# MLP of a two-layer decoder trunk: Strassen product sums kept over the passes, a quarter of two more column blocks by Strassen, and PSUM banks named

## The chip, the core and the metric

The kernel runs on one core of a Trainium2 chip. The metric is device time in microseconds (us) of one execution, the median of several runs. The engines are PE (TensorE: matrix products), DVE (VectorE), ACT (ScalarE), POOL (GpSimd) and SP (SyncE, which here only issues transfers). PE writes its results to PSUM, eight banks of 128 partitions x 512 float32 numbers each; the other memory on the core is SBUF.

## The reference, cut to what matters

The model has two layers on one sequence of 256 positions with 2048 features. Layer 0 mixes by a gated short convolution, layer 1 by latent attention. Both have the same MLP behind the mixer, with its own weights, and a layer norm after every part:

```
def sq_relu_mlp(x, w1, w2):                    # w1: 2048 x 8192, w2: 8192 x 2048
    return jnp.square(jax.nn.relu(x @ w1)) @ w2

h = layer_norm(ALPHA * h + mix, ...)
h = layer_norm(ALPHA * h + sq_relu_mlp(h, mlp_w1[layer], mlp_w2[layer]), ...)
```

All data are float32.

## The kernel before, in words

**Numbers as pairs.** For a matrix product, each float32 operand is split in two parts, hi and lo, of the type fp32r. `split` (L114) does this: ACT writes hi by a cast (L116), DVE writes lo = x - hi (L117). A product a b is then taken as hi hi + hi lo + lo hi. With activations as the stationary operand and weights as the moving one, that is three matmuls of 512 columns, written by `dot` (L274 to L278). With weights as the stationary operand, one 512-column matmul takes hi of the weights against hi and lo of x side by side (`high`, L192), and one 256-column matmul takes lo against hi (`low`, L196).

**Weights.** All weights come through one list, `stream`, in tiles of 128 x 1024 (512 KB). `take` (L166) hands out the next ones and has `prepare` (L130) load and split tiles up to LOOK = 5 ahead. There are five buffers for raw tiles and eight each for hi and lo. The order of instructions on an engine follows the order of the program only roughly: the framework's scheduler places an instruction when its inputs and buffers are expected to be ready.

**The MLP** (`mlp`, L557) goes in 8 passes, q = 0 to 7. In a pass, `products` (L265) computes 8 chunks of 128 hidden features (16 K tiles each, ps_u), and `hidden` (L593) evicts each (`whole`, L329 to L333), applies the squared ReLU and splits the result. Then the down stage multiplies the pass's 8 chunks (K tiles, taken in 4 pairs) with the matching rows of w2 and adds the result to `acc`, which holds 2 row halves t x 4 column blocks n of 512. Pass 0 also finishes the norm before the MLP; in pass 7 the blocks go on to the next norm (`to_wide`) or to the output (`to_out`).

In passes 1 to 6 (FAST) the column blocks 0 and 1 are computed by Strassen's scheme in Winograd's form: per K pair, 7 factors in place of 8 block products (`down_fast`, ps_f). The weight side of the factors is made in `prepare` from two raw tiles (L130 to L160): three splits of 1024 columns, one of 512 (the tile t4), one subtraction of 1024 (L149) and two of 512 (L152, L155). The activation side is made in `hidden`: four sums of 128 columns (L605 to L608) and a split into `forms`. After four K pairs `combine` (L642) adds the seven products to `acc`, with 11 operations on DVE and one on ACT. Blocks 2 and 3 are computed plainly by `down` (L288): per K pair and block 2 x 2 x 3 = 12 matmuls (ps_d), and one addition to `acc` per row half (L581).

**Banks.** `psum` (L180) takes a PSUM tile from one of two pools of four buffers; a pool gives any free buffer. The second pool is closed in the attention part, where other tiles use its banks, and opened again after it (`banks = Banks.open("second")`), where `out_chunks` runs the rest of the attention's output projection (ps_l) behind its first three accumulators (ps_wo, `first_o`).

**Other lines that the text names.** `Norm.prepare` (L389) subtracts a mean taken from chunk 0, for which it needs one float32 matmul (mu0p, L396); `begin` calls it for all 16 chunks at the start of pass 7 of the first MLP. `residual` (L486, through L493) adds an accumulator to xres in two halves. `turn_residual` transposes the residual into `acc` in passes 1 to 4 of the second MLP. TURNED swaps `high` and `low` at the third K tile of a pass's first product. `to_out` loads the last gain and bias, gbt, by POOL's queue; the tables cos_t, sin_t and mask_t are loaded after the convolution.

Of the kernel before, what the change touches and what calls it, by code (L numbers as in the profile page):

```python
# [16 lines left out]
P = 128  # L17
# [5 lines left out]
NQ = 8  # L23
# [13 lines left out]
FAST = range(1, NQ - 1)  # L37
FIRST = (0, 1, 2, 4, 6, 8, 12, 16)
# [12 lines left out]
def trunk(ctx: ExitStack, tc: tile.TileContext, xT, vecs, w_first, w_in, w_out, w_kv, w_q, w_uk, w_uv,  # L51
          w_qn, w_qp, w_o, w1, w2, w2f, cosT, sinT, mask, ident, gb, out):
# [8 lines left out]
    pmm = ctx.enter_context(tc.tile_pool(name="pmm", bufs=4, space=PS))  # L61
# [12 lines left out]
    def mlp_stream(l):  # L74
        out = []
        for q in range(NQ):
            out += halves(w1[l, q * QC:(q + 1) * QC])
            lead = 0
            if q in FAST:
                out += [(w2f[l, q, j, 0], w2f[l, q, j, 1]) for j in range(QC // 2)]  # L80
                lead = 2
            out += halves(w2[l, q, lead:])
        return out
# [6 lines left out]
    class Banks:  # L90
# [4 lines left out]
        @classmethod  # L95
        def open(cls, name):
            st = ExitStack()
            cls.more, cls.count = st.enter_context(tc.tile_pool(name=name, bufs=4, space=PS)), 0
            return st
# [80 lines left out]
    def psum(name):  # L180
        return Banks.next().tile([P, 512], F32, tag="mm", name=name)
# [83 lines left out]
    def products(n, x, turned=None):  # L265

        for i in range(n):
            w = take()
            ps = psum("ps_u")
# [30 lines left out]
    def down_late(x, put, blocks):  # L300

        ws = {}
        for t in range(2):
            for n in blocks:
# [11 lines left out]
    def down_fast(x, forms):  # L316

        ps = {p: psum(f"ps_f{p}") for p, _, _ in FACTORS}
        n = len(x) // 2
        for j in range(n):  # L320
            b, = take(1)
            a = {"11": held(x[2 * j], 0), "12": held(x[2 * j + 1], 0), "22": held(x[2 * j + 1], 1)}
            for i in range(4):
                a[f"S{i + 1}"] = [forms[:, j, o, i * P:(i + 1) * P] for o in range(2)]
            for p, l, r in FACTORS:
                dot(ps[p], b[r], a[l], j == 0, j == n - 1)
        return ps
# [14 lines left out]
    cos_t = const.tile([P, T], F32, name="cos_t")  # L342
    sin_t = const.tile([P, T], F32, name="sin_t")
    mask_t = const.tile([P, 3 * P], F32, name="mask_t")
# [9 lines left out]

    def late_constants():
        nc.sync.dma_start(id_t, ident)
        nc.sync.dma_start(cos_t, cosT)
        nc.sync.dma_start(sin_t, sinT)
        nc.sync.dma_start(mask_t, mask)
# [193 lines left out]
    late_constants()  # L553
# [3 lines left out]
    def mlp(idx, ln, blocks, fast, begin=None, extra=None):  # L557
# [24 lines left out]

        for q in range(NQ):
# [5 lines left out]
            if q == NQ - 1 and begin:  # L589
                begin()  # L590
            pair = []

            def hidden(m, ps, evac, *func):  # L593
                f = tmp.tile([P, T], F32, tag="fh", name="fh", bufs=3)
# [4 lines left out]
                put_split(h[m], f)  # L599
                pair.append(f)  # L600
                if forms is not None and m % 2:
                    (a11, a21), (a12, a22) = ((v[:, :P], v[:, P:]) for v in pair[-2:])
# [8 lines left out]
            if q == 0:  # L611
                for m in range(QC):
# [12 lines left out]
                    if m > 0:  # L625
                        normal()
                acc = act.tile([P, 2, D], F32, tag="a1", name=f"acc{idx}")
            else:
                for m, ps in enumerate(products(QC, xhl, turned=None if q == NQ - 1 and begin else TURNED)):
                    hidden(m, ps, whole)  # L630

# [10 lines left out]
    def combine(put, p):  # L642

        put(0, 1, p["4"])
        put(0, 0, p["2"])
        put(1, 0, p["3"])
        v, u = (raws.tile([P, 2, BW], F32, tag="raw", name="vu")[:, i, :] for i in range(2))
        put(0, 0, p["1"])
        nc.scalar.copy(v, p["1"])
        nc.vector.tensor_tensor(v, v, p["6"], ALU.add)  # L650
        nc.vector.tensor_tensor(u, v, p["7"], ALU.add)
        put(1, 0, v)
        put(0, 1, u)
        put(1, 0, p["5"])
        put(1, 1, u)
        put(1, 1, p["5"])
# [23 lines left out]
    def prepare_all():  # L680
        for k in range(NC):
            ln.prepare(k)

    with tc.tile_pool(name="fast1", bufs=1) as fast:
        mlp(1, before, to_wide, fast, begin=prepare_all)


    with tc.tile_pool(name="att", bufs=1) as ap:
        lat = act.tile([P, 2 * NK, 2 * T], F32R, tag="c", name="lat")
        chl, qhl = ([lat[:, k, :] for k in range(o, o + NK)] for o in (0, NK))  # L690
        kpe = ap.tile([P, 2, T], F32, name="kpe")
# [6 lines left out]
        def rope(dst, src, rows):  # L698

            a = tmp.tile([P, T], F32, tag="sq", name="ropea")  # L700
            b = tmp.tile([P, T], F32, tag="nu", name="ropeb")
# [201 lines left out]
    def turn_residual(block, n):  # L903
        if 0 <= n < NB:
            for t in range(2):
                ps = psum("turned")
                for j in range(4):
# [155 lines left out]
```

## Time and profile before

| what | us |
|---|---|
| median of 3 runs (2032.22 to 2032.32) | 2032.28 |
| the profiled execution | 2031.86 |
| its span, first to last instruction | 2030.0 |
| PE busy, by the page | 2022.8 |
| DVE busy | 1637.1 |
| ACT busy | 1186.2 |
| bytes read from HBM | 381.25 MB |

The page's first part gives busy times. PE's is close to the span, but matmuls are pipelined and a busy PE need not be PE at its peak, so PE must also be read in order of time. In the same execution PE's work goes through these stages (start in us): first MLP, pass 1 products 454.47, Strassen part 498.86, plain part 518.45; pass 2 products 540.25; pass 7 products 969.4, down stage 1013.97; attention 1115.88 to 1249.77; second MLP, pass 1 products 1412.96; pass 7 products 1931.24, down stage 1975.63, last matmuls 2025. The granted clock of TensorE is 1.00 throughout. A row of the timeline shows start, length, engine, line, operation, what it writes and reads, and how many were merged into the row; in brackets, the idle time before it and what ended it.

### The profile page before, as it was taken

The numbers are of one execution on the slowest core, as the hardware profiler recorded it, in microseconds if no ns is written. First come the engines' busy times: TensorE is split into PE (matmuls) and PEld (weight loads), VectorE is DVE, ScalarE is ACT, GpSimd is POOL, SyncE is SP. The second block draws the span as 40 slices with busy tenths as digits, with TensorE's granted clock in tenths as the row PEclk, the third lists the DMA queues.
The fourth block names the chain that finished last, engine by engine and source line by source line (L and its number), as shares of the span: only waits on it lengthen the run. The fifth ranks groups of instructions, "written<-read, shape, count | busy, mean of one in ns | idle before, by whom it ended". The sixth has DMA issues, their size and how long they took to land.

```text
span 2030.0 us, 30192 instructions
## 1 busy us (share of the span) xinstructions
PE 2022.8 (100%) x11240; PEld 1763.4 (87%) x11240; DVE 1637.1 (81%) x2559; ACT 1186.2 (58%) x1849; POOL 4.5 (0%) x25
## 2 busy tenths in 40 slices
PE   9999999999999999999999999999999999999998
PEld 8888888988888888888889998898888888888886
DVE  7667677778898988989788978776889898898966
ACT  6444445676566565655656655566656656565661
POOL 0000000000000000000000000000000000000000
PEclk9999999999999999999999999999999999999999
DMA  8666666564746557465654544656474664746573
GB/s 307 209 191 187 188 190 193 162 210 138 251 148 216 193 170 256 145 229 174 232 176 153 177 129 137 195 168 205 136 240 155 213 204 164 250 143 221 190 228 121
DMA packets 106851, 385.32 MB, mean 190 GB/s; under 512 B 11856, under 2 KB 12752, under 8 KB 106448
## 3 DMA queue, kind: packets, MB, share of 16 engines
q1 hardware_dynamic: 105984, 381.17, 57.9%
q0 software_dynamic: 576, 2.10, 0.3%
q8 instruction: 88, 1.44, 0.3%
q14 instruction: 59, 0.48, 0.1%
q10 hardware_dynamic: 144, 0.13, 0.0%
HBM read 381.25 MB, written 2.10 MB: 189 GB/s over the span
## 4 chain that ended last, share of the span: by engine, by line
PE 99%; DMA 0%; DVE 0%; issue 0%; SPq 0%; ACT 0%; DVEq 0%
PE ps_u L192 20%; PE ps_l L192 13%; PE ps_u L196 11%; PE ps_d L276 7%; PE ps_d L277 7%; PE ps_d L278 7%; PE ps_l L196 7%; PE ps_f L278 4%; PE ps_f L276 4%; PE ps_f L277 4%; PE ps_w L226 1%; PE ps_w L224 1%; PE ps_w L225 1%; PE ps_g L226 1%; PE ps_g L224 1%; PE ps_g L225 1%
## 5 line engine op out<-in xcount | busy, mean ns | idle before, releaser
L117 DVE TENSOR_TENSOR lo<-raw,hi 128x1024 fp32r<-128x1024 f32 x710 | 858.7, 1222 | 271.5 <-ACT hi L116 199.9
L116 ACT CAST hi<-raw 128x1024 fp32r<-128x1024 f32 x710 | 740.9, 1050 | 428.4 <-DMA raw<-in_w_dram 134.6
L192 PE MATMUL ps_u<-xhl,hi 128*128 128x512 f32 x1792 | 621.3, 391 | 0.0
L196 PE MATMUL ps_u<-xhl,lo 128*128 128x256 f32 x1792 | 500.1, 280 | 0.0
L192 PEld LDWEIGHTS ps_u<-xhl,hi 128*128 128x128 f32 x1792 | 334.4, 187 | 71.9
L196 PEld LDWEIGHTS ps_u<-xhl,lo 128*128 128x128 f32 x1792 | 339.2, 189 | 1.7
L276 PE MATMUL ps_d<-hi,h 128*128 128x512 f32 x640 | 249.9, 390 | 0.0
L277 PE MATMUL ps_d<-lo,h 128*128 128x512 f32 x640 | 249.3, 390 | 0.0
L278 PE MATMUL ps_d<-hi,h 128*128 128x512 f32 x640 | 249.2, 389 | 0.0
L192 PE MATMUL ps_l<-xhl_a,hi 128*128 128x512 f32 x704 | 244.1, 393 | 0.0
L196 PE MATMUL ps_l<-xhl_a,lo 128*128 128x256 f32 x704 | 195.5, 280 | 0.0
L192 PEld LDWEIGHTS ps_l<-xhl_a,hi 128*128 128x128 f32 x704 | 132.2, 188 | 29.8
L278 PEld LDWEIGHTS ps_d<-hi,h 128*128 128x128 f32 x640 | 120.2, 188 | 25.2
L276 PEld LDWEIGHTS ps_d<-hi,h 128*128 128x128 f32 x640 | 120.2, 188 | 25.0
L277 PEld LDWEIGHTS ps_d<-lo,h 128*128 128x128 f32 x640 | 120.2, 188 | 24.6
L196 PEld LDWEIGHTS ps_l<-xhl_a,lo 128*128 128x128 f32 x704 | 131.9, 188 | 0.2
L597 ACT ACTIVATE fh<-fh 128x256 f32<-128x256 f32 x112 | 46.5, 415 | 89.2 <-DVE fh L333 89.1
L116 ACT CAST hi_t<-raw_t 128x1024 fp32r<-128x1024 f32 x48 | 50.6, 1054 | 55.5 <-DVE raw_t L149 30.5
L192 PE MATMUL ps_l<-z,hi 128*128 128x512 f32 x240 | 82.4, 391 | 0.0
L226 PE MATMUL ps_w<-xd,hi 128*128 128x258 f32 x256 | 72.7, 285 | 0.0
L224 PE MATMUL ps_w<-xd,hi 128*128 128x258 f32 x256 | 72.6, 284 | 0.0
L225 PE MATMUL ps_w<-xd,lo 128*128 128x258 f32 x256 | 72.4, 283 | 0.0
(253 smaller groups left out, 3185.1 us busy)
## 6 DMA issues: line engine op xcount, KB each, us to landing
raw<-in_w_dram SPq DMA_DIRECT2D x416, 512.0 KB, 4.3
raw<-in_w2f_dram SPq DMA_DIRECT2D x96, 512.0 KB, 3.5
raw<-in_w_in_dram SPq DMA_DIRECT2D x88, 512.0 KB, 3.8
raw<-in_w_out_dram SPq DMA_DIRECT2D x32, 512.0 KB, 3.6
raw<-in_w_o_dram SPq DMA_DIRECT2D x32, 512.0 KB, 4.0
raw<-in_w_kv_dram SPq DMA_DIRECT2D x10, 512.0 KB, 3.6
raw<-in_w_q_dram SPq DMA_DIRECT2D x8, 512.0 KB, 4.4
raw<-in_w_uk_dram SPq DMA_DIRECT2D x8, 512.0 KB, 4.6
```

The lines of the kernel that those rows point to most:

```text
L116: nc.scalar.copy(hi, src)
L117: nc.vector.tensor_tensor(lo, src, hi.bitcast(F32), ALU.subtract)
L192: nc.tensor.matmul(ps, w[blk // 8][0][:, blk % 8, :], x, start=first, stop=False)
L196: nc.tensor.matmul(ps[:, :T], w[blk // 8][1][:, blk % 8, :], x[:, :T], start=False, stop=last)
L224: nc.tensor.matmul(ps[:, :W], hi, x[k][:, :W], start=k == 0, stop=False)
L225: nc.tensor.matmul(ps[:, :W], lo, x[k][:, :W], start=False, stop=False)
L226: nc.tensor.matmul(ps[:, :W], hi, x[k][:, W:], start=False, stop=k == NC - 1)
L276: nc.tensor.matmul(ps, x[0], w[0], start=first, stop=False)
L277: nc.tensor.matmul(ps, x[0], w[1], start=False, stop=False)
L278: nc.tensor.matmul(ps, x[1], w[0], start=False, stop=last)
L597: nc.scalar.activation(f, f, AF.Relu)
```

## The change

1. In passes 1 to 6, one of the four K pairs of blocks 2 and 3 (the third: MIXED = "ppsp") is computed by the seven factors; the other three stay plain. Weights for it come in a new array w2g, in the same bytes.
2. The products are no longer combined in every pass. Each product has a place where it is summed over the passes: 1, 5, 7 and 6 in a new tile `sums`, 2, 3, 4 and the plain sum 22 in `acc` (`keep`). `fold` adds them up once per MLP, in 8 operations of 1024 columns during the products of pass 7.
3. Every PSUM tile has a bank by number. Tiles without a named bank take the next number of a count, modulo 8, or 4 while the second pool is closed. The products of passes 1 to 7 alternate between banks 0 and 1; the factors take 2 to 7 and 0, in the order 3, 1, 5, 7, 2, 6, 4.
4. Two chunks of hidden features are split together (512 columns) in passes 1 to 6.
5. The mean's matmul and chunk 0 of `begin` go to the end of pass 0's products; the other chunks go one or two at a time behind the products of pass 7. `turn_residual` runs after the first K pair of the plain part. Only pass 1 keeps the turned order.
6. For room in SBUF, the three tables are loaded when attention starts, gbt is loaded by SP's queue, and the scratch for POOL's transfers is made smaller.

```
+MIXED = "ppsp"
...
-    pmm = ctx.enter_context(tc.tile_pool(name="pmm", bufs=4, space=PS))
+    pmm = ctx.enter_context(tc.tile_pool(name="pmm", bufs=1, space=PS))
...
         def next(cls):
             cls.count += 1
-            return cls.more if cls.more is not None and cls.count % 8 >= 4 else pmm
+            return (cls.count - 1) % (4 if cls.more is None else 8)
...
-    def psum(name):
-        return Banks.next().tile([P, 512], F32, tag="mm", name=name)
+    def psum(name, bank=None):
+        bank = Banks.next() if bank is None else bank
+        return (pmm if bank < 4 else Banks.more).tile([P, 512], F32, tag=f"mm{bank}", name=name)
...
-    FACTORS = (("4", "22", "T4"), ("2", "12", "21"), ("3", "S4", "22"), ("1", "11", "11"),
-               ("6", "S2", "T2"), ("7", "S3", "T3"), ("5", "S1", "T1"))
+    OWN, KEPT = ("1", "5", "7", "6"), (2, 3, 4, 5, 6, 7, 0)
+    FACTORS = (("3", "S4", "22"), ("1", "11", "11"), ("5", "S1", "T1"), ("7", "S3", "T3"),
+               ("2", "12", "21"), ("6", "S2", "T2"), ("4", "22", "T4"))
...
+        def keep(p, g, ps):
+            at = sums[:, OWN.index(p), g, :] if p in OWN else \
+                block(*{"2": (2 * g, 0), "3": (2 * g + 1, 0), "4": (2 * g, 1), "22": (2 * g + 1, 1)}[p])
+            if q == 1 and p in OWN:
+                nc.scalar.copy(at, ps)
+            else:
+                nc.vector.tensor_tensor(at, at, ps, ALU.add)
+
+        def down_pairs(h, forms):
+            n = QC // 2
+            ps = {p: psum(f"ps_f{p}", bank) for (p, _, _), bank in zip(FACTORS, KEPT)}
+            for j in range(n):
+                fast_products(ps, h, forms, j, ps if j == 0 else (), ps if j == n - 1 else ())
+            for p in ps:
+                keep(p, 0, ps[p])
+            ps = {p: psum("ps_d", bank) for p, bank in zip(("22", "3", "2", "4"), (1, *KEPT))}
+            for j, kind in enumerate(MIXED):
+                if kind == "s":
+                    first, last = j == MIXED.index("s"), j == MIXED.rindex("s")
+                    if first:
+                        ps.update({p: psum(f"ps_f{p}", bank) for p, bank in zip(OWN, KEPT[3:])})
+                    fast_products(ps, h, forms, j, OWN if first else (), OWN if last else ())
+                    if last:
+                        for p in OWN:
+                            keep(p, 1, ps[p])
+                    continue
+                for nb, two in ((3, ((1, "22"), (0, "3"))), (2, ((0, "2"), (1, "4")))):
+                    w, = take(1)
+                    for t, p in two:
+                        for kk in range(2):
+                            k = 2 * j + kk
+                            dot(ps[p], wide_rows(w, kk), held(h[k], t), k == 0, k == QC - 1)
+                if extra and q <= NB and j == 0:
+                    for t in range(2):
+                        extra(block, q - 1, t, KEPT[4 + t])
+            for p in ("3", "2", "4", "22"):
+                keep(p, 1, ps[p])
+
+        def fold():
+            s1, s5, s7, s6 = (sums[:, i] for i in range(4))
+            c = acc.rearrange("p t (g b c) -> p t b g c", g=2, b=2)
+            for d, a, b in ((c[:, 0, 0], c[:, 0, 0], s1), (s6, s6, s1), (c[:, 0, 1], c[:, 0, 1], s6), (s7, s7, s6),
+                            (c[:, 1, 0], c[:, 1, 0], s7), (c[:, 1, 1], c[:, 1, 1], s7),
+                            (c[:, 0, 1], c[:, 0, 1], s5), (c[:, 1, 1], c[:, 1, 1], s5)):
+                nc.vector.tensor_tensor(d, a, b, ALU.add)
+                yield
...
-                for m, ps in enumerate(products(QC, xhl, turned=None if q == NQ - 1 and begin else TURNED)):
+                folds = fold()
+                for m, ps in enumerate(products(QC, xhl, TURNED if q == 1 else None, (0, 1))):
                     hidden(m, ps, whole)
+                    if q == NQ - 1:
+                        next(folds)
+                        if begin:
+                            begin(range(max(2 * m, 1), 2 * m + 2))
...
             if q in FAST:
-                combine(put, down_fast(h, forms))
-            for n in range(2 if q in FAST else 0, NB):
-                if n == NB - 1 and extra:
-                    extra(block, q - 1)
-                down(h, put, n)
+                down_pairs(h, forms)
+            else:
+                for n in range(NB):
+                    down(h, put, n)
...
-            nc.gpsimd.dma_start(gbt[:, n, :], gb[n].partition_broadcast(P))
+            nc.sync.dma_start(gbt[:, n, :], gb[n].partition_broadcast(P))
```

More of the change, by code (lines that the diff above doesn't have):

```diff
@@ L263, in opening, with products @@
         yield from [ps for _, ps in ws]
[L265 removed]
+    def products(n, x, turned=None, banks=(None,)):
         for i in range(n):
             w = take()
[L269 removed]
+            ps = psum("ps_u", banks[i % len(banks)])
             mm_run([(w, ps)], x, 0, NC, NC, turned=None if i else turned)
```

113 lines of the change are left out of this document (53 added, 60 removed).

## The prediction, made before the changed kernel ran

> **What bounds the kernel now.** I read the page's busy times first, then the chain that ended last, the waits of PE, and then PE's instructions in order of time.
>
> ```profile
> span 2030.0 us, 30192 instructions
> ...
> PE 2022.8 (100%) x11240; PEld 1763.4 (87%) x11240; DVE 1637.1 (81%) x2559; ACT 1186.2 (58%) x1849; POOL 4.5 (0%) x25
> ...
> PE 99%; DMA 0%; DVE 0%; issue 0%; SPq 0%; ACT 0%; DVEq 0%
> ```
>
> PE is busy for the whole span and is 99% of the chain. The four waits of PE that the profile names come to 3.2 us, and none lies in an MLP pass. So only fewer or faster matmuls can help, and any new wait of PE costs its full length. But the 390 ns of a matmul in the groups is latency, not price: the next one starts long before it ends. The price is the distance from start to start.
>
> ```profile
> 498.86 0.39 PE L276 MATMUL ps_f<-t,h 128*128 128x512 f32 x1
> ...
> 518.45 0.40 PE L276 MATMUL ps_d<-hi,h 128*128 128x512 f32 x1
> ...
> 540.25 0.39 PE L192 MATMUL ps_u<-xhl,hi 128*128 128x512 f32 x1
> ```
>
> These are the first Strassen matmul of pass 1 of the first MLP, its first plain one (ps_d) and the first product of pass 2. Between them lie 84 Strassen matmuls, 19.59/84 = **0.2332 us** each, and 96 plain ones, 21.80/96 = **0.2271 us** each. (At 390 ns each removed matmul would count 1.7 times.) A pass is 44.39 + 19.59 + 21.80 = 85.78 us, and the passes between repeat this to 0.02 us (the second MLP has 0.9 us more in four of them, for transposes). There are 12 such passes (q 1 to 6, twice). The next question is what DVE has left in each stage of a pass:
>
> ```profile
> 626.03:670.42 44.39, 44.39 (x257) 39.17 (x256) 36.79 (x57) 29.07 (x49) 0.00 (x0) 1.00 0.51 166
> 670.42:690.01 19.59, 19.59 (x86) 15.78 (x85) 18.38 (x26) 12.47 (x18) 0.00 (x0) 1.00 0.60 193
> 690.01:711.81 21.80, 21.80 (x98) 18.02 (x96) 19.32 (x23) 10.87 (x11) 0.00 (x0) 1.00 0.76 252
> ```
>
> The rows are products, Strassen part and plain part of pass 3; after the length come the busy times of PE, PEld, DVE, ACT and POOL. DVE is idle for 7.6, 1.2 and 2.5 us. The cover is there, but in the Strassen part it is thin.
>
> **Step 1, the removed matmuls.** One of four K pairs of blocks 2 and 3 goes from 2 x 2 x 2 x 3 = 24 plain matmuls to 7 x 3 = 21. At the rows' prices this is 24 x 0.2271 - 21 x 0.2332 = 5.450 - 4.897 = 0.553 us a pass, 12 x 0.553 = **-6.6 us**. The changed order (six plain matmuls to a bank, the factor T4 last) has no row. If the new Strassen matmuls ran at the plain price, 3 x 0.2271 x 12 = -8.2 us. If all 72 plain ones of a pass rose to the Strassen price, 12 x 72 x 0.0061 = 5.3 us would be lost again and -1.3 us left. I take -6.6, each kind at its own row. The Trainium skill, "TensorE: Matmul & The Clock Gate", section "Wait — 56ns, not 53.3ns?", gives one spacing of 215.7 ns for all warm 512-column matmuls; by it step 1 would be an estimated 36 x 0.2157 = 7.8 us. The trace has two spacings, both longer.
>
> **Step 2, DVE in a pass.** Back to back, an operation of 1024 columns takes 1.14 us (four in a row 4.63 us, one 1.22), of 512 columns 0.60 (two 1.28, one 0.68), of 256 columns 0.34 (four 1.43, one 0.42). Removed: two plain splits (2.27), 11 operations of combine and 4 puts. Added: a Strassen pair, 4 x 1.14 + 3 x 0.60 = 6.35, and 15 keeps in place of those 15 operations. The split by pairs gives 4 x 0.60 for 8 x 0.34, -0.3. Net +3.8 us: from 74.5 to 78.3 us in a pass of 85.2. It fits on the whole, so I cost it at nothing; the work that hides it is PE's. In the part after the first four pairs DVE needs 19.3 + 4.1 = 23.4 us against 21.2 of PE. The 2.2 us over spill into the next products, which have 7.6 to spare, and eight hi/lo buffers carry them. The mixed pair sits third, so PE wants its first factor 2 x 5.45 = 10.9 us after the first four pairs and its last, T4, 4.2 us later, at 15.1. From that start DVE owes 7 keeps (4.2), one plain split (three already ran in the last 5 us of the Strassen part: 684.47, 3.69 us for three) and for the first factor one split of the pair: 4.2 + 1.1 + 1.1 = 6.4 of 10.9 us; for all of the pair 4.2 + 1.1 + 6.35 = 11.7 of 15.1. ACT gains about 1 us on 52.4 and stays clear. If the cover is gone, each us late costs 12.
>
> **Step 3, the banks.** Products now have two banks, so the eviction of product m must end within one product, 5.55 us. In the passes shown here the eviction (L333) ends 2.1 to 4.0 us after its product. Of the first keeps, the banks of 3, 1 and 5 are wanted again 1.4, 2.7 and 4.1 us after the Strassen part ends; today the first three evictions end 1.3 us before, 1.6 and 3.3 us after it. The slack is 1.5, 1.1 and 0.8 us. In four passes of the second MLP the transposes want the fifth and sixth at 5.45 and 5.85 us; at 0.6 us a keep they end near 4.5 and 5.1. So nothing, but barely.
>
> One bank does collide. Before, a slot is taken from a pool of four; afterwards the number is a count modulo 4 or 8, set to 0 when the second set of banks opens. Counted through the code, 49 tiles in the convolution, 16 in its output, 19 in q 0 of the first MLP (the mean's included), 19 in q 7, 10 in the latent stage, 49 in attention: 162. The three w_o accumulators are 163 to 165, banks 2, 3 and 0; the next product is tile 1 of the new count, bank 0. It has to wait for the third accumulator's eviction.
>
> ```profile
> 1249.64 0.28 PE L196 MATMUL ps_wo<-oT,lo 128*128 128x256 f32 x1
> 1249.77 1.99 PE L192 MATMUL ps_l<-oT,hi 128*128 128x512 f32 x8
> ```
>
> ```profile
> 1249.26 1.43 DVE L493 TENSOR_TENSOR xres<-xres,ps_wo 128x256 f32<-128x256 f32 x4 [1.56 <-PE ps_wo L196]
> ...
> 1250.81 0.41 DVE L493 TENSOR_TENSOR xres<-xres,ps_wo 128x256 f32<-128x256 f32 x1
> ...
> 1251.47 0.42 DVE L493 TENSOR_TENSOR xres<-xres,ps_wo 128x256 f32<-128x256 f32 x1
> ```
>
> PE goes on at 1249.77 today; the last read of the third accumulator ends at 1251.89. The wait is 2.1 us, once: **+2.1**. Bounds: 0 if PE has the bank already, 2.5 with the signal's way. Behind it PE has only matmuls of that stage.
>
> **Step 4, what moves.** The mean's matmul (mu0p) goes from the start of q 7 to the end of q 0. Today a product's first pair after it takes 0.42 us instead of 0.23 (969.40 to 969.82); a plain matmul after transposes takes 0.32 (1036.56 to 1036.88). So -0.1. Unit 0 of q 2 to 7 loses its turned order; no row shows the unturned one after ps_d. From 0 (no gap there to win) to 0.19 x 11 = +2.1, the gap after mu0p as upper end; I take 0, since the gap stands only behind 32-bit matmuls. The fold is 8 x 1.14 = 9.1 us of DVE in each q 7, one step to a product: splits 2.3 + evictions 0.7 + step 1.1 + two prepares 0.7 = 4.8 of 5.55 us. The four loads of gbt go to SP's queue, where they wait for the last product (1975.6) with weight loads behind them. At that moment SP issues the 11th of q 7's 16 plain tiles, 30 us ahead of PE at 2.73 us a tile; gbt lands in 7.4 to 12.4 us. Nothing; if SP reached them six tiles earlier, about 1 us. The tables cos, sin and mask load (4.9 us) into memory that is free before q 7's down stage and are used 50 us later.
>
> **Sum.** -6.6 + 2.1 - 0.1 = -4.6 us. The profiled execution took 2031.86 (span 2030.0 and 1.8 around it) and gives 2027.3; the median of the runs is 0.4 higher, so 2032.3 - 4.6 = **2027.7**. About 0.2% (4.1 us, the line is 2028.2) is what a measurement of this kernel can tell from no change, and the forecast lies just past it.
>
> **Rivals.**
> - **A, the forecast**: 2027.7, own range 2026 to 2029.8. 0.55, of which 0.42 below 2028.2.
> - **B, no wait at w_o**, or Strassen at the plain price: 2032.3 - 6.7 = 2025.6, down to 2024. For: DVE may do the third accumulator's adds first. Against: the row above. 0.13.
> - **C, a wait in every fast pass**: the mixed pair's weights, or a bank, come late. For: DVE has 1.2 us idle in the Strassen part, and the tightest slack above is 0.8 us, at a bank. Against: the pair has 3.4 us to spare, and today's passes run at this density without a wait. 1.0 us late in each gives 12 more: 2039.7. It decides from 4.6/12 = 0.38 us a pass on; from 0.72 the kernel is slower by over 0.2%. 0.15. By the section "A second HAM failure mode: psum-queue depth-cycling" of the same page of the Trainium skill, short idle times between groups that cycle through banks also let the clock drop; here the clock is 1.00 in all three rows, and that time would come on top.
> - **D, unturned starts**: +2.1, 2029.8. 0.05.
> - **E, the removal does not pay**: the plain matmuls take the Strassen price, -1.3 + 2.0 = 2033. For: the reason of the 6 ns is not in the trace. Against: plain matmuls keep 0.2271 in all passes. 0.12, of which 0.09 within 0.2%.
>
> Faster 0.42 + 0.13 = 0.55; within 0.13 + 0.05 + 0.09 = 0.27; slower 0.15 + 0.03 = 0.18. The range goes from 2023.5 (all of B) to 2034.5 (past E); C is left out.
>
> **What would show it.** A pass should be 85.2 us, 44.4 + 19.6 + 21.2, without a gap in PE (A, B) or with one at the mixed pair, at a bank's first matmul or at the third product (C). Between ps_wo and ps_l PE should stand 2.1 us. The start distances decide E, unit 0 of a pass decides D. I would be wrong above all if PE waits in every pass.

## The result, and the profile after

The changed kernel takes 2036.57 us (median of 15 runs, 2034.0 to 2040.39), the kernel before 2031.88 us beside it (15 runs, 2031.42 to 2033.58). The ratio is 1.0024, with a 95% interval of 1.0016 to 1.0032: slower by about 0.2%, and outside the range of the prediction. The profiled execution took 2035.76 us.

The page of the changed kernel, its first part and its chain:

```profile
span 2034.0 us, 30032 instructions
...
PE 2025.4 (100%) x11204; PEld 1756.3 (86%) x11204; DVE 1686.9 (83%) x2571; ACT 1198.7 (59%) x1829; POOL 2.3 (0%) x21
...
PE 93%; DVE 4%; DMA 1%; issue 1%; ACT 1%; DVEq 0%; ACTq 0%
```

There are 36 matmuls fewer (11204 for 11240), and PE is busy for 2.6 us longer. So the rest must have become dearer. DVE and the transfers now have 5% of the chain, so PE waits for them here and there. The waits of PE, as engine, line and releaser, then us in total, times, longest:

```profile
PE ps_u L199 <- DVE sums L588: 1.9, 3, 1.0
PE offset L1011 <- DVE udiag L1009: 1.4, 1, 1.4
PE warm L353 <- DVE col L355: 1.1, 1, 1.1
PE ps_d L283 <- DVE sums L588: 0.2, 1, 0.2
```

The first and the last row are new. There PE wants a bank whose keep (L588) DVE has not finished. With PE's rows in order of time these are five gaps in the second MLP, 2.9 us in all. That is less than the span grew, so the next view is the length of each stage. Stretches of the changed kernel (products, Strassen part and the rest of pass 2, then the attention's projection behind ps_wo); after the length come the busy times of PE, PEld, DVE, ACT and POOL, the clock, DMA share and GB/s:

```profile
539.94:585.15 45.21, 45.21 (x257) 39.23 (x256) 38.70 (x58) 27.69 (x45) 0.00 (x0) 1.00 0.54 171
585.15:604.64 19.49, 19.49 (x87) 15.81 (x86) 17.74 (x24) 12.85 (x17) 0.00 (x0) 1.00 0.62 193
604.64:625.90 21.26, 21.26 (x94) 17.47 (x93) 20.30 (x24) 11.08 (x12) 0.00 (x0) 1.00 0.69 238
1250.38:1323.77 73.39, 73.39 (x419) 63.72 (x418) 59.99 (x100) 40.95 (x59) 0.00 (x0) 1.00 0.61 190
```

and two of the same stages before:

```profile
540.25:584.64 44.39, 44.39 (x257) 39.17 (x256) 37.35 (x59) 28.88 (x49) 0.00 (x0) 1.00 0.52 166
1249.77:1321.89 72.12, 72.12 (x419) 63.59 (x418) 59.29 (x100) 40.89 (x59) 0.00 (x0) 1.00 0.61 194
```

The down stage got shorter as meant, 19.49 + 21.26 = 40.75 for 41.39 us. But the products, 256 matmuls of which the change touches only the banks and the order of two at the start, take 45.21 for 44.39, with PE busy throughout, no wait and a clock of 1.00. The attention's projection, where only the banks changed, takes 73.39 for 72.12. The sum over the profiled execution:

| what | us |
|---|---|
| 12 down stages, 0.64 shorter each | -7.7 |
| 9 product stages of 14 at 45.2 to 45.3, some 0.82 longer each | +7.4 |
| projection behind ps_wo | +1.3 |
| five waits for keeps in the second MLP | +2.9 |
| sum (the span grew by 4.0) | +3.9 |

**Two rhythms.** Most of the gain was eaten by a rhythm of PE. These are the distances from start to start that the trace holds for the beginning of pass 2, in ns; the bar is the first product, L marks a 256-column matmul (`low`), the others have 512 columns:

```
before ... 226 227 227 | 226 114L 232 118L 121L 237 235 117L 235 116L 230 117L 230 117L ...
after  ... 227 226 227 | 227 113L 233 117L 241 120L 236 113L 233 117L 241 120L 236 113L ...
```

Both start alike. Before, the third K tile is turned (low ahead of high), and after two more pairs all pairs are 230 + 117 = 347 ns, or 1 ns less; their mean is 346.7 ns. Unturned, three pairs of 349, 350 and 361 ns repeat to the end of the stage; the mean is 353.3 ns. 128 pairs x 6.6 ns = 0.85 us, close to the row's 0.82. I call them the short and the long rhythm.

### The profile page after: what moved, and what is told of

Same layout as the page of the kernel before. It is cut to its first block, busy times and chain, and to the rows that moved or that the text cites. A ratio compares the mean times of both kernels' runs of the same rounds, so it can differ in the third digit from the quotient of the medians.

```text
span 2034.0 us, 30032 instructions
## 1 busy us (share of the span) xinstructions
PE 2025.4 (100%) x11204; PEld 1756.3 (86%) x11204; DVE 1686.9 (83%) x2571; ACT 1198.7 (59%) x1829; POOL 2.3 (0%) x21
## 4 chain that ended last, share of the span: by engine, by line
PE 93%; DVE 4%; DMA 1%; issue 1%; ACT 1%; DVEq 0%; ACTq 0%
PE ps_u L199 20%; PE ps_l L199 13%; PE ps_u L203 10%; PE ps_l L203 7%; PE ps_d L283 6%; PE ps_d L285 6%; PE ps_d L284 6%; PE ps_f L283 3%; PE ps_f L285 3%; PE ps_f L284 3%; PE ps_w L233 2%; PE ps_w L231 2%; PE ps_w L232 2%; DMA raw<-in_w_dram 1%; DVE lo L122 1%; PE ps_g L233 1%
## 5 line engine op out<-in xcount | busy, mean ns | idle before, releaser
L199 PE MATMUL ps_u<-xhl,hi 128*128 128x512 f32 x1792 | 629.6, 396 | 1.9 <-DVE sums L588 1.9
L283 PE MATMUL ps_d<-hi,h 128*128 128x512 f32 x556 | 217.5, 391 | 0.2 <-DVE sums L588 0.2
L285 PE MATMUL ps_d<-hi,h 128*128 128x512 f32 x556 | 216.6, 390 | 0.0
L284 PE MATMUL ps_d<-lo,h 128*128 128x512 f32 x556 | 216.6, 390 | 0.0
L121 ACT CAST hi_t<-raw_t 128x1024 fp32r<-128x1024 f32 x60 | 63.0, 1050 | 108.8 <-DVE raw_t L154 93.3
L283 PEld LDWEIGHTS ps_d<-hi,h 128*128 128x128 f32 x556 | 104.4, 188 | 22.6 <-DVE sums L588 0.7
L285 PEld LDWEIGHTS ps_d<-hi,h 128*128 128x128 f32 x556 | 104.4, 188 | 22.1
L284 PEld LDWEIGHTS ps_d<-lo,h 128*128 128x128 f32 x556 | 104.4, 188 | 21.7
L652 ACT ACTIVATE fp<-fp 128x256 f32<-128x256 f32 x96 | 40.0, 417 | 81.5 <-DVE fp L338 80.7
L154 DVE TENSOR_TENSOR raw_t<-raw,raw 128x1024 f32<-128x1024 f32 x60 | 73.1, 1219 | 7.4 <-DMA raw<-in_w2f_dram 7.3
L122 DVE TENSOR_TENSOR lo_t<-raw_t,hi_t 128x1024 fp32r<-128x1024 f32 x60 | 73.2, 1220 | 1.3
L233 PE MATMUL ps_w<-xd,hi 128*128 128x258 f32 x256 | 72.9, 285 | 0.0
```

Source lines behind the costliest of these rows:

```text
L121: nc.scalar.copy(hi, src)
L122: nc.vector.tensor_tensor(lo, src, hi.bitcast(F32), ALU.subtract)
L154: nc.vector.tensor_tensor(t.rearrange(two, a=2), b12.unsqueeze(1).to_broadcast([P, 2, BW]), r1.rearrange(two, a=2), ALU.subtract)
L199: nc.tensor.matmul(ps, w[blk // 8][0][:, blk % 8, :], x, start=first, stop=False)
L233: nc.tensor.matmul(ps[:, :W], hi, x[k][:, W:], start=False, stop=k == NC - 1)
L283: nc.tensor.matmul(ps, x[0], w[0], start=first, stop=False)
```

## The experiments

Theory S: the long rhythm, which an unturned start out of the even stream of plain matmuls (227 ns each) falls into, eats the gain. Theory W: the waits for late keeps do. Times are medians, with the range and the number of runs; ratios are to the kernel before, on the same chip, with a 95% interval. Of a changed line, only the part that differs is shown; `...` stands for lines left out.

**1. All passes turned again.**

```
-products(QC, xhl, TURNED if q == 1 else None, (0, 1))
+products(QC, xhl, TURNED, (0, 1))
```

> The changed kernel with the turned order kept for the first product of every pass from 1 to 7, not of pass 1 alone. Theory S (spacing): products that start unturned straight after 512-column matmuls run a whole stage at 45.21 us, turned ones at 44.39; all 14 product stages then read 44.4. In the profile of the changed kernel 9 stages were slow, so -9 x 0.82 = -7.4 us: 2036.6 becomes about 2029. Theory W (waits): the loss is PE waiting for late keeps at the end of passes of the second MLP, 2.8 us in the profile and more in other runs; turning changes nothing there, 2036.6 +- 1, and the scatter over the runs (2034 to 2040) stays.

2034.22 us (2031.27 to 2037.41, 11 runs), ratio 1.0009 (1.0 to 1.0018). This lies between the two. Eleven of the 14 stages are at 44.4 to 44.5 us, so turning does what S says; but gaps of 3.7 us stay, and three stages of the first MLP (passes 5 to 7) are still long. Passes 4 and 5, as stretches:

```profile
711.15:755.54 44.39, 44.39 (x257) 39.11 (x256) 39.50 (x58) 29.42 (x47) 0.00 (x0) 1.00 0.54 187
796.30:841.52 45.22, 45.22 (x257) 39.21 (x257) 40.49 (x59) 30.01 (x47) 0.00 (x0) 1.00 0.57 189
```

Both are turned. In the second one, two distances at the start are 3 to 4 ns longer. Its first two pairs are already those of the short rhythm, and the same turn leads out of it into the long one:

```
pass 5 ... 227 227 230 | 231 117L 230 117L 118L 232 231 114L 232 118L 240 120L 236 114L ...
```

So the rhythm hangs on the phase at which the turn meets it, and S and W are not independent: pass 7 is long behind a wait of 0.1 us.

**2. Another order of banks for the mixed pair's products**, so that bank 0, which the next products want first, holds the product whose keep comes first.

```
-zip(OWN, KEPT[3:])
+zip(("6", "5", "7", "1"), KEPT[3:])
```

> The changed kernel with one pair of banks exchanged: of the mixed pair's own products, the one that is kept first (1) takes bank 0, which the next pass's first product needs, and the one kept last (6) takes bank 5. Theory W: the waits of PE for keeps at the start of passes go, 2.8 us or more, and the runs scatter less: about 2033. Theory S: without a gap ahead of them, passes 3, 4 and 6 of the second MLP fall into the slow spacing too, 3 x 0.76 = 2.3 us, so the gain is eaten: 2036 +- 1, with 12 of 14 product stages at 45.2 us.

2036.58 us (2034.89 to 2037.41, 11), 1.0021 (1.0012 to 1.003). No gain, as S said. The waits ahead of the products are gone; but 12 stages are now long where there were nine, since a wait ahead of an unturned start had put it into the short rhythm three times. What the removed waits had cost, the longer stages took. Of the waits that stay, the two longer ones (0.6 and 1.2 us) lie in the plain part, for bank 3, the first keep of product 1; one of 0.16 us lies at the second product of a pass.

**3. The change without its mixed pair.** All four pairs plain; the second half of `sums` is zeroed.

```
-MIXED = "ppsp"
+MIXED = "pppp"
+        nc.gpsimd.memset(sums[:, :, 1, :], 0.0)
```

> The changed kernel with all four K pairs of blocks 2 and 3 plain (sums of the mixed pair set to zero once and folded like the others). It isolates the mixed pair. If its three matmuls fewer are worth what the plain part showed (21.26 us in place of 21.80, 0.54 a pass), passes lose 12 x 0.54 = 6.5 us. DVE has 4 us less a pass, so by W the waits of 2.8 us go: 2036.6 + 6.5 - 2.8 = 2040. By S the second MLP's stages behind those waits turn slow as well, +2.3: 2042.5. If mixing itself were the loss, the time would fall below 2036.

2042.13 us (2041.42 to 2045.0, 5), 1.0053 (1.0039 to 1.0067). As S says, 12 of 14 stages are at 45.21, and the gaps come to 0.24 us in all. The long rhythm does not need the mixed pair. And the mixed pair is worth its saving where nothing waits: a pass of the first MLP with the long rhythm takes 86.48 us here and 85.96 us in the changed kernel.

**4. The kernel before, unturned.**

```
-turned=None if q == NQ - 1 and begin else TURNED
+turned=TURNED if q == 1 else None
```

> The kernel before with one edit: only pass 1 keeps the turned order. Theory S: 11 more stages start unturned (pass 7 of the first MLP already did, behind the 32-bit matmul of the mean) and each goes from 44.39 to 45.21 us: 2031.9 + 11 x 0.82 = 2040.9. The prediction's upper end for this edit was 0.19 x 11 = 2.1, 2034. Theory W: no late keeps in this kernel, no change, 2031.9.

2040.34 us (2040.12 to 2042.87, 5), 1.0043 (1.0031 to 1.0056), where S expected 2040.9. The products of pass 2:

```profile
540.25:585.46 45.21, 45.21 (x257) 39.16 (x256) 38.26 (x60) 29.62 (x50) 0.00 (x0) 1.00 0.52 170
```

One edit, which adds no instruction, costs 8.3 us: eleven stages are at 45.21. In the traces the order of instructions on DVE and ACT is that of the kernel before, and on PE only the swaps differ. So S is shown in a kernel that has nothing else of the change.

**5. The change mended:** turned everywhere, the banks of 2, and fixed banks for ps_wo, so that the first ps_l is not blocked.

```
-first_o.append((take(), psum("ps_wo")))
+first_o.append((take(), psum("ps_wo", (2, 3, 1)[i])))
+                Banks.count += 2
```

> The changed kernel with three edits: turned order in every pass, the exchange of banks 0 and 5 among the mixed pair's products, and banks 2, 3 and 1 for the three w_o accumulators so that the next product finds bank 0 free. If slow spacing and late keeps together are the whole loss: 9 stages back to 44.4 (-7.4), w_o stage back from 73.4 to 72.1 (-1.3), part of the 2.8 us of waits: 2036.6 - 8.7 - 1 = 2027. What the earlier run with the turned order alone leaves open is whether a wait of a few ns ahead of a turned start also leads to the slow spacing; if so, up to four stages stay at 45.2: 2030. If the loss lies elsewhere, it stays above 2034.

2032.55 us (2028.18 to 2033.6, 11), 0.9997 (0.9988 to 1.0006). All 14 stages are at 44.39 and the projection is at 72.12 again, yet the time is that of before. In the profiled execution, the shortest of the eleven, the new row among PE's waits is:

```profile
PE ps_d L283 <- DVE sums L588: 2.1, 4, 1.1
```

PE's rows show 3.0 us of such gaps, each some 2.7 us behind a Strassen part, where bank 3 is wanted. So W has a share of its own. The median is 4.4 us above this execution, and the scatter is 5 us; that the other executions wait more is likely but not shown, since only one was traced.

**6. The mixed pair in the first MLP alone** (`MIXED if idx == 1 else "pppp"`, in the stream too).

> As the run before it, but the mixed pair is used in the first MLP only; in the second all four K pairs of blocks 2 and 3 are plain. Late keeps were seen almost only in the second MLP, where DVE also adds the residual. Expected: passes of 85.1 us in the first MLP (6 x -0.64 against the kernel before), 85.7 and 86.6 in the second (6 x -0.1 for the factor order) without waits: 2031.9 - 3.8 - 0.6 + 0.4 = 2027.9, with little scatter. If late keeps do not come from DVE's load, waits remain in the second MLP and the time is near 2031.

2031.28 us (2029.22 to 2032.42, 11), 0.9993 (0.9984 to 1.0002). A miss: there are waits of up to 0.9 us in both MLPs, and one stage is long; it starts short and changes behind a wait of 0.27 us at its second product. The waits are not bound to the second MLP's transposes. Nor do they need the mixed pair's work on DVE: the second MLP, which has none here, waits 0.7 us in one pass.

**7. Blocks in another order:** the two tiles of block 3 of the first two pairs ahead of both of block 2, so that bank 3 is wanted later.

```
-                else:
-                    out += halves(w2[l, q, 3, j]) + halves(w2[l, q, 2, j])
+                elif j != 1:
+                    js = (0, 1) if j == 0 else (j,)
+                    for n in (3, 2):
+                        for i in js:
+                            out += halves(w2[l, q, n, i])
...
```

> As the mended kernel, but of the first two plain pairs both tiles of block 3 come before both of block 2, so that banks 3 and 4 are wanted 2.7 us later. The waits left with the bank exchange alone (0.6 and 1.2 us) stood 2.5 us after the Strassen part, where bank 3 waits for the keep of product 1. If that deadline was the cause they go, and with them the slow stages: 2025.5. If DVE is simply too full in the down stage, they move on to the next bank: no gain against the mended kernel.

2031.2 us (2027.97 to 2034.1, 11), 0.9994 (0.9985 to 1.0003). No gain that can be measured. The matmuls of `down_pairs` follow the same order. Most of PE's waits went elsewhere, to the banks of the transposes' additions:

```profile
PE ps_f L286 <- DVE acc L967: 2.4, 4, 1.1
```

Two more, of 0.6 us each, lie at the second product of a pass, one of them for a split of weights. Where a bank's date is moved, another is late. So it is DVE that is behind for a time, not one bank that is placed badly.

**8. The phase of the turn.** The kernel before, turned at K tile 3 in passes 2 to 6 of the first MLP and at K tile 5 in the second. If the long rhythm is a cycle of three pairs, a turn ends it at its third pair (2 or 5) and not at its first (3).

```
-turned=None if q == NQ - 1 and begin else TURNED
+turned=None if q == NQ - 1 and begin else TURNED if q == 1 else 3 if idx == 1 else 5
```

> The kernel before with the turned K tile moved in passes 2 to 7: from the third to the fourth in the first MLP (5 stages), to the sixth in the second (6 stages). The slow spacing repeats every three K tiles. If a turn helps only at one point of that cycle, the sixth (three later) works as the third does, and stages stay at 44.4, while the fourth leaves the stages of the first MLP slow: 2031.9 + 5 x 0.82 = 2036. If any turn ends the slow spacing, all stages read 44.4 and the time stays 2032.

2036.3 us (2036.12 to 2038.35, 10), 1.0021 (1.0012 to 1.003). The phase decides. Pass 2 of the first MLP and pass 3 of the second:

```profile
540.59:585.80 45.21, 45.21 (x257) 39.23 (x256) 37.58 (x59) 29.36 (x49) 0.00 (x0) 1.00 0.52 171
1592.13:1636.54 44.41, 44.41 (x257) 39.12 (x256) 36.52 (x57) 29.17 (x49) 0.00 (x0) 1.00 0.53 171
```

```
K tile 3 | 227 113L 232 118L 241 120L 120L 236 233 113L 233 117L 241 120L 236 113L ...
K tile 5 | 227 113L 232 118L 241 120L 236 113L 232 118L 121L 237 235 117L 235 117L 230 116L ...
```

All five stages turned at 3 are long, all six turned at 5 short. The 0.02 us between 44.41 and 44.39 are the one cycle passed through first. The attention's projection, which the edit does not touch, takes 73.48 us in this trace: with the banks of the kernel before, it is in the long rhythm too.

**9 to 11. Seven raw buffers, seven pairs of hi and lo** (`RAW, WA = 7, 7`), if the splits stand waiting for tiles that have not landed: the mended kernel (9), with the order of 7 (10), and the kernel before as control (11).

> The mended kernel with seven raw buffers in place of five and seven hi/lo pairs in place of eight (the same space). Theory L (landing): in the changed kernel's second MLP DVE stood idle 1.6 us for ACT, and ACT 2.1 us for a weight tile to land, with keeps queued behind on DVE; a transfer can only start when one of five raw buffers is free, and 4.5 us pass until it lands. With two more in flight these waits shrink: the median falls from 2032.5 towards 2027 and the runs scatter less than the 5 us of the mended kernel. Theory F (full): DVE simply has too much to do in the down stage; then nothing improves, and one hi/lo pair less makes it worse, 2033 or more.

> The same seven and seven buffers with both tiles of block 3 first. Theory L: 2031.2 falls to about 2026. Theory F: 2031 or more, and the waits stand at the mixed pair's banks as before.

> Control: the kernel before with seven and seven buffers. PE has no wait in its passes, so both theories expect 2032 +- 1; if it falls, the buffers are worth something by themselves and the two runs ahead of it have to be read against this.

9: 2031.72 us (2030.06 to 2035.02, 11), 0.9999 (0.999 to 1.0008). 10: 2030.83 us (2029.54 to 2035.11, 11), 0.9997 (0.9988 to 1.0006). 11: 2042.01 us (2041.32 to 2042.7, 4), 1.005 (1.0035 to 1.0065), where 2032 was expected. This decides nothing, and the control says why: the kernel before, which has no such waits, loses 10 us by the same edit, so it has a price of its own (in 9, the stretch from the last products to the end takes 103.4 us for 98.8). In the first MLP of 9 all passes take 85.14 us, with no wait.

**12. The mended kernel with all pairs plain** (the edit of 3).

> The mended kernel with all four K pairs of blocks 2 and 3 plain (the unused sums set to zero): what keeping the sums and naming the banks is worth without the mixed pair. All stages at 44.4 us, w_o at 72.1; the factor order gives 0.1 us a pass, -1.2, and the mean's move +0.3: 2031.1, scatter as in the kernel before. If the banks or the keeps cost something by themselves, it stays above 2032.

2032.34 us (2031.69 to 2034.88, 11), 1.0003 (0.9994 to 1.0012). With good starts, sums, fold and banks together cost nothing and bring nothing: a pass without a wait takes 85.66 us for 85.78, and gaps of 1.6 us in the second MLP take this back. The longest of them are waits for keeps too, without the mixed pair's work. The median of 5 (2032.55) is no lower, so there the mixed pair's saving was lost again; its trace shows 3.0 us of waits, the rest is not traced.

**13 and 14. What makes DVE late.** Theory L (landing): the keeps stand in DVE's queue behind splits of tiles that have not landed. Theory F: DVE has too much to do. 13 takes transfers away (every second w1 tile from pass 1 on is not loaded), 14 takes work off DVE in the mixed pair (`light` holds for it alone): it leaves out two subtractions and one lo part.

```
-            out += halves(w1[l, q * QC:(q + 1) * QC])
+            units = halves(w1[l, q * QC:(q + 1) * QC])
+            out += [(None,) if q and i % 2 else u for i, u in enumerate(units)]
...
-            raw = load_raw(i, stream[i][0])
+            raw = state["raw"] = state["raw"] if stream[i][0] is None else load_raw(i, stream[i][0])
```

```
-        finished(t, f"{i}_t")
-        nc.vector.tensor_tensor(b12, b22, t[:, :BW], ALU.subtract)
+        if light:
+            hi = whl.tile([P, 8, P], F32R, tag="hi", name=f"hi{i}_t")
+            nc.scalar.copy(hi, tiled(t))
+            out.append((hi, out[0][1]))
+        else:
+            finished(t, f"{i}_t")
+            nc.vector.tensor_tensor(b12, b22, t[:, :BW], ALU.subtract)
...
-        nc.vector.tensor_tensor(t4, b21, b12, ALU.subtract)
+        if not light:
+            nc.vector.tensor_tensor(t4, b21, b12, ALU.subtract)
```

> The mended kernel with every second weight tile of the MLP products in passes 1 to 7 not loaded: its split reads the raw tile before it once more. This leaves out half of w1 in these passes. Instructions of PE, DVE and ACT are the same; only transfers are fewer, 8 of 32 tiles' worth a pass. Theory L (keeps wait behind splits whose tiles have not landed): the waits and the scatter go, 14 stages at 44.4 and passes at 85.1: 2031.9 - 7.7 + 0.3 = 2024.5, scatter about 1 us. Theory F (DVE has too much to do): no change, 2032.5 with 5 us of scatter.

> The mended kernel with less work for DVE in the mixed pair: two subtractions of 512 columns and one split of 1024 are left out (the pair's factors are then not the right ones), 2.3 us of DVE a pass in the down stage; transfers are the same. Theory F: waits and scatter go, 2024.5 to 2026. Theory L: the tiles land as late as before, the waits stay in most passes: 2030 to 2032.

13: 2024.15 us (2024.03 to 2024.8, 5), 0.9957 (0.9944 to 0.9969), and no gap. 14: 2024.99 us (2024.43 to 2025.34, 5), 0.996 (0.9947 to 0.9972), gaps of 0.8 us. Each theory had bet that the other's lever would do nothing; both levers work, so neither holds alone. The rows show how the two are tied. DVE, ACT and PE of the changed kernel around the start of pass 5 of the second MLP (each row: start, length, then the instruction, and in brackets the idle time before it):

```profile
1757.05 1.23 DVE L122 TENSOR_TENSOR lo<-raw,hi 128x1024 fp32r<-128x1024 f32 x1 [1.62 <-ACT hi L121]
1758.19 0.68 DVE L588 TENSOR_TENSOR sums<-sums,ps_f 128x512 f32<-128x512 f32 x1
1758.79 1.22 DVE L122 TENSOR_TENSOR lo<-raw,hi 128x1024 fp32r<-128x1024 f32 x1
1759.92 1.87 DVE L588 TENSOR_TENSOR sums<-sums,ps_f 128x512 f32<-128x512 f32 x3
```

```profile
1755.96 1.05 ACT L121 CAST hi<-raw 128x1024 fp32r<-128x1024 f32 x1 [2.13 <-DMA raw<-in_w_dram]
```

```profile
1760.84 0.39 PE L285 MATMUL ps_d<-hi,h 128*128 128x512 f32 x1
1761.94 0.47 PE L199 MATMUL ps_u<-xhl,hi 128*128 128x512 f32 x1 [0.72 <-DVE sums L588]
```

ACT stands 2.13 us for a transfer, so DVE stands 1.62 us for ACT, with the four keeps behind that split and the next. The last keep ends at 1761.79, PE would have gone on at 1761.07 and goes on at 1761.94. But by the program a transfer can only start when DVE's split has freed one of the five raw buffers, and the waits of SP's queue in the changed kernel show it:

```profile
SPq L132 <- DVE lo L122: 858.7, 417, 16.1
```

Transfer, cast and split make a loop, and a DVE that is late makes the next landing late.

**15 to 18. A sixth raw buffer**, with all eight hi/lo pairs; its room comes from the scratch for POOL's transfers. 15 is the mended kernel, 16 that with the order of 7, 17 the change as it was, 18 the kernel before.

```
-RAW, WA = 5, 8
+RAW, WA = 6, 8
...
-nc = _bacc.Bacc("TRN2", target_bir_lowering=False, num_devices=1, dynamic_dma_scratch_size=4096)
+nc = _bacc.Bacc("TRN2", target_bir_lowering=False, num_devices=1, dynamic_dma_scratch_size=256)
```

> The mended kernel with six raw buffers in place of five and all eight hi/lo pairs; the room comes from the scratch for POOL's transfers, which nothing uses any more. Theory L: one more tile in flight shortens the waits, 2032.5 falls to 2026 to 2029. Theory F: 2032.5.

> The same with both tiles of block 3 ahead of both of block 2. Theory L: 2025 to 2028. Theory F: 2031.

> The changed kernel with the sixth raw buffer alone: no turned order, banks as changed. It tells the two losses apart in the changed kernel itself. If six buffers end the late keeps, no wait is left in the passes; but then no wait breaks the slow spacing any more, and 12 of 14 product stages read 45.2 (three more than in the profile of the changed kernel), with w_o at 73.4: 2023.9 + 12 x 0.82 + 1.3 = 2035, with 1 us of scatter. If the waits were the main loss, it falls to about 2026.

> Control: the kernel before with six raw buffers (and half the scratch for POOL's transfers). Its passes have no wait to lose, so 2032 +- 0.7. If it falls, the sixth buffer's gain is not the changed kernel's alone.

15: **2023.86 us** (2023.63 to 2023.89, 5), 0.9955 (0.9942 to 0.9967). It beats both kernels, and the scatter of 5 us has shrunk to 0.3. Its page, its waits of PE and the two parts of pass 3:

```profile
span 2022.1 us, 30013 instructions
...
PE 2014.6 (100%) x11204; PEld 1755.5 (87%) x11204; DVE 1677.7 (83%) x2571; ACT 1199.3 (59%) x1829; POOL 2.3 (0%) x21
```

```profile
PE ps_g L199 <- ACT hi L121: 1.2, 1, 1.2
PE offset L1012 <- DVE udiag L1010: 1.2, 1, 1.2
PE warm L353 <- DVE col L355: 1.1, 1, 1.1
```

```profile
625.46:669.85 44.39, 44.39 (x257) 39.12 (x256) 36.18 (x54) 26.28 (x42) 0.00 (x0) 1.00 0.51 168
669.85:710.60 40.75, 40.75 (x179) 33.28 (x178) 40.28 (x51) 25.91 (x32) 0.00 (x0) 1.00 0.65 222
```

No wait is left in the passes, all 14 stages are short, and a pass is 44.39 + 40.75 = 85.14 us. DVE is busy for 40.28 of the 40.75 us of the down stage: full, but never late. ACT's waits for weights have halved; from the mended kernel's waits of ACT

```profile
ACT hi L121 <- DMA raw<-in_w_dram: 120.0, 134, 2.7
```

and from those of 15:

```profile
ACT hi L121 <- DMA raw<-in_w_dram: 57.7, 86, 2.4
```

16: 2025.87 us (2025.74 to 2026.82, 5), 0.9966 (0.9952 to 0.9979); the order of 7 keeps 1.3 us of waits at ps_f and is not needed.

17: 2034.9 us (2034.43 to 2037.12, 11), 1.0014 (1.0005 to 1.0023), with no gap, 12 long stages and 73.4 us in the projection, as expected. Beside 15 this is S by itself: 2034.9 - 2023.86 = 11.0 us, and 12 x 0.82 + 1.3 = 11.1. DVE and ACT have the same order of instructions in both traces.

18: 2041.09 us (2039.64 to 2042.55, 4), 1.0047 (1.0031 to 1.0062), where 2032 was expected. The waits of PE there:

```profile
PE ps_d L276 <- DVE acc L581: 5.1, 8, 0.9
```

In DVE's rows the scheduler now puts two splits (602.60 and 604.35) ahead of the addition of product sums that the kernel before has at 602.27. These waits are 5.1 of the 7.9 us by which this trace is longer. The number of buffers also rewrites the order of instructions on DVE and ACT. So 15 could owe its gain over 5 to another order, and 13 and 14 as well, since the order on DVE differs from that of 5 in each. For 13 and 15 the traces allow one more step. Counted from a pass's last eviction of a product, in passes 2 to 6 of both MLPs, and at 1.14, 0.60 or 0.34 us an operation by its size, DVE has as much work ahead of every keep as in 5, or more (up to 2.2 us in 13, 4.0 us in 15). So the keeps did not get better places; the work ahead of them ended in time. Whether in 15 the sixth buffer alone did that, or the other order of splits and casts has a part in it, stays open.

## Why the prediction was wrong

**Step 1 was right**, and a little small: -0.64 us a pass, 12 times, is -7.7 where I had -6.6. Of the 0.64, the mixed pair gives 0.54 (21.26 for 21.80), as counted; the 0.10 in the Strassen part (19.49 for 19.59) came with the new order of factors and banks, for which I had no row; no run separates the two. The new order did not make plain matmuls dearer (rival E): Strassen part and plain part take 19.49 + 21.26 for the 19.6 + 21.2 that I named.

**The step that failed is step 4**, in the words "Unit 0 of q 2 to 7 loses its turned order; no row shows the unturned one after ps_d. From 0 ... to 0.19 x 11 = +2.1 ... I take 0". I priced the start as one gap. It is a switch between two rhythms that hold for all 256 matmuls of a stage: 0.82 us each, +7.4 us in the profiled execution and 9.8 (12 stages) where no wait disturbs a start. Rival D had the place, but a quarter of the price and a chance of 0.05. The bound was not a bound, since it came from a row of another kind, a gap behind 32-bit matmuls. And the trace of before held the long rhythm: two full cycles of it in the last ps_wo, right ahead of the row that I quoted for the collision (distances 241, 120, 236, 113, 233 ns). I had read those rows for their ends only. The one unturned stage of the kernel before, pass 7 of the first MLP, gave no warning: it starts behind the mean's matmul with that gap of 0.42 us and goes straight into the short rhythm.

**Step 2 and step 3 were right in sum and wrong in effect.** DVE's time in a pass is 38.70 + 17.74 + 20.30 = 76.7 us in pass 2, below my 78.3. But I set work against time as if each instruction could start when DVE was free. Keeps stand behind splits, and splits wait for landings; of the waits that follow, the largest came at a bank whose date I had not worked out, bank 0, which holds a product of the mixed pair and is wanted 24 x 0.2271 = 5.45 us after it. "Nothing, but barely" was five waits in four of the twelve passes, 2.9 us in the profiled execution or 0.24 us a pass: rival C's mechanism, below the 0.38 from which it decides. In the dates of step 3 the first slack is 1.4 + 1.3 = 2.7 us, not 1.5. The second, 1.1 us at the bank of product 1, is the one that runs 2 and 5 exceed (waits of up to 1.3 us).

**The collision at w_o was there, its price was not.** I expected PE to stand 2.1 us. The order of the instructions was written with the collision in it, by putting the start of a later tile ahead of the blocked one. PE's rows behind ps_wo:

```profile
1250.38 1.99 PE L199 MATMUL ps_l<-oT,hi 128*128 128x512 f32 x8
1252.21 0.28 PE L203 MATMUL ps_l<-oT,lo 128*128 128x256 f32 x1
1252.32 0.40 PE L199 MATMUL ps_l<-oT,hi 128*128 128x512 f32 x1
1252.55 0.28 PE L203 MATMUL ps_l<-oT,lo 128*128 128x256 f32 x1
1252.67 2.26 PE L199 MATMUL ps_l<-oT,hi 128*128 128x512 f32 x9
```

The row of nine holds one matmul of the tile before it and the eight of the blocked tile, 2.5 us after the stage's first. PE does not stand between ps_wo and ps_l. But from this start all but the first part of the stage falls into the long rhythm: +1.3 us. With the banks named otherwise (5) the stage takes 72.12 again. A blocked bank is not the only way into it, as run 8 shows, and in 10 the stage takes 73.49 us with the banks of 5, behind a delay of some 0.1 us in its first tile.

**The rest held**: the fold, the loads of gbt and the tables cost nothing that the trace shows; the mean's move gives back in pass 7 about the 0.3 us that it costs in pass 0. The granted clock is 1.00 in every stretch shown, so a lower clock is not the cause of the longer stages.

With the starts, the banks and the waits all mended (15), the span is 2022.1, and 2030.0 - 7.7 = 2022.3: what the shorter down stages alone give.

## What to carry to other kernels

Where PE is the bound, compare the distances from start to start of a stage that the change does not touch, over hundreds of matmuls, before and after: an edit at the first few instructions can change the rate of all that follow. A price taken from a row of another kind is a guess and no bound, and an edit that "only" drops an ordering trick should be run alone on the kernel before. When DVE or ACT is busy for nearly all of a stage (here DVE for 38 of 40.75 us of the down stage), look at what stands behind an instruction that waits for a transfer, and at whether that transfer waits for the same engine; and run any new number of buffers on the unchanged kernel too, since it rewrites the order.

## What the runs showed of the hardware that was not expected

- The same sequence of weight loads and matmuls (512 columns, 256 columns, and so on) has two steady rhythms at one clock of 1.00: 347 ns a pair, and a cycle of three pairs (349, 350, 361 ns). One short stage of the changed kernel (pass 6 of the second MLP) alternates 350 and 343 ns instead, with the same mean. Without a wait or a swap each holds to the end of its stage, 128 pairs. A swap of two neighbours ends the long one at the third pair of its cycle (K tiles 2 and 5) and not at its first (K tile 3). A start that is 3 to 4 ns late can be in the short one by itself, and then the swap ends that (run 1).
- The Trainium skill says, in the section "Back-to-back issue gap" of "TensorE: Matmul & The Clock Gate", that in a stream of weight loads and matmuls both together set the spacing. That would leave room for two rhythms of one sequence, but its 131 ns for 512 columns is far below the 227 to 241 ns measured here; which of PE's resources makes the cycle, no run here shows.
- A wait of PE ahead of an unturned start brought the short rhythm three times of four in the profiled execution, and the shortest of these waits, 0.16 us, saved 0.76 us of the stage behind it (44.45 for 45.21).
